# Opening of the even layer: input weights by quarters between conditioning quarters, fillers on TensorE, R multiplied into x ahead

## The chip, the cores and the metric

The kernel runs on one core of one Trainium2 chip. The metric is device time in microseconds (us). PE is TensorE (PEld its weight loads), DVE VectorE, ACT ScalarE, POOL GpSimd, SP SyncE, which issues the transfers (DMAs).

## The reference

Two layers of a diffusion backbone over 512 latent tokens of 1024 channels, all fp32. What matters here is the start of layer 0:

```python
m_lat = (jax.nn.silu(c) @ mod_w[l] + mod_b[l])[:, None, :]
sh1, sc1, g1, sh2, sc2, g2 = jnp.split(m_lat, 6, axis=-1)
h_lat = rms_norm(x, pre_mix_g[l]) * (1 + sc1) + sh1
m_ctx = jax.nn.silu(c_ctx) @ mod_w[l] + mod_b[l]
...
h_ctx = rms_norm(ctx, pre_mix_g[l]) * (1 + csc1) + csh1
...
pl = jnp.split(h_lat @ w_in, EVEN_OFFSETS, axis=-1)   # q, kv, rope key, gla q, k, v, gates, output gate
pc = jnp.split(h_ctx @ w_in, EVEN_OFFSETS, axis=-1)
```

So the first projections need, for each of eight chunks of 128 channels, the norm of x (over all chunks) and two conditioning vectors (a scale A and a shift S for x, A0c and S0c for the 256 context tokens), which come out of a product of c with a 1024 x 2048 part of `mod_w`.

## The kernel before

Activations lie transposed, channels on partitions, tokens along the free dimension: x is eight tiles of 128 x 512, ctx eight of 128 x 256. An fp32 product is made of three fp32r products: every operand is split into a high part (`hi`, a cast on ScalarE) and a low part (`lo`, the rest, a subtraction on VectorE or GpSimd), and `kstep` adds hi x hi, lo x hi and hi x lo. Weights come as units of 128 x 1024 (512 KB), each holding all eight k-chunks of 128 outputs; `unit` loads a few units ahead into four `raw` buffers and splits them.

The opening runs from the first loads to the last product with the first four units: rg (rope keys and gate ranks), kv, gq0 and gq1. Its products are written as `wave(ks, w, js)`: for k-chunks ks, for the latent (w = 0) or context tokens (w = 1), units js. The conditioning product is done in four quarters q, each for the two k-chunks 2q and 2q + 1 of x: `cond_load(q)` loads 2 MB in eight pieces (tiles `mw`, or `raw` for the first quarter and the end of the fourth), `cond` multiplies them (32-column products), `cond_done` copies the row out (tile `mrow`), turns it with two thin products against `sel` and makes A, S, A0c, S0c of two chunks. Then `latent(c)` and `context(c)` make `hl` and `hc` with `modulate`: VectorE makes x * A * R, ScalarE adds S for the high part, VectorE makes the low part. R is the rms factor of x, spread over partitions by PE (`rms_sum`, `rms_spread`; the power is GpSimd's).

Before, the four units are loaded whole after the first conditioning quarter, and each conditioning product of the later quarters is cut in two, with waves between the halves.

The class `ordered` keeps the instructions of an engine in the order in which they are written while its `on` is set: before, PE and SP in the opening. Everywhere else a scheduler decides the order from the program and its own model. SP issues transfers in order, and an issue waits where its buffer is not yet free; PSUM has two `big` buffers and four `one` buffers.

Behind the opening come gk0 and gk1 (`two`), beside which VectorE sums modulation vectors from `mraw` loads (`mod_steps`, tiles `macc`), then a run of thin products: the sum of squares of kv (`kvq`), the doubling of the rope key (`tk`, `dup`), four gates (`gin` x `wz` in `log_gates`, 32 rows), then units q0, q1, gv0 to gv3, gr0 and on. The log gates `lg` feed the linear attention: scans on VectorE (`bf`, `cb`), exponentials on ScalarE and products on GpSimd (`q`, `ek`, `ke`, `ec`), beside GpSimd's weight splits.

## Time and profile before

| | |
|---|---|
| median of 3 runs | 1357.37 us (1352.23 to 1358.7) |
| profiled execution | 1357.05 us, span 1355.2 us |
| busy, share of the span | PE 96%, PEld 78%, DVE 54%, ACT 40%, POOL 39% |
| opening's input products, first to last | 22.16 to 66.8 us |
| mean granted clock over the span | 0.985 |

The granted clock has two levels: 1.00 is 2.4 GHz, 0.50 is 1.2 GHz. In timeline rows x is the number of instructions merged, and the bracket is the idle time of the engine ahead of the row and what ended it. An fp32 (not fp32r) product counts twice there.

### The profile page before, as it was taken

The page shows a single profiled execution, that of the slowest core. Times are in us where ns is not written, and L with a number is a line of the kernel's source. Part 1 is how long each engine was busy: PE and PEld are TensorE (multiplying, and loading weights), DVE is VectorE, ACT ScalarE, POOL GpSimd, SP SyncE. Part 2 cuts the span into 40 slices and gives each one's busy share as a digit, 9 for nine tenths or more (in the row PEclk, how much of TensorE's full clock was granted, in tenths as well). Part 3 has the DMA queues.
Part 4 walks back from the last instruction along what each step waited for, and adds up shares of the span by engine and source line. Part 5 has one row for each costly group of instructions (what it writes and reads, how often), then busy time and mean ns, then how long its engine had stood idle before and what let it go on. Part 6 is the DMA issues. An engine that isn't in the chain of part 4 may idle for free.

```text
span 1355.2 us, 19529 instructions
## 1 busy us (share of the span) xinstructions
PE 1301.6 (96%) x7602; PEld 1052.9 (78%) x7602; DVE 734.6 (54%) x1132; ACT 546.9 (40%) x964; POOL 522.4 (39%) x352
## 2 busy tenths in 40 slices
PE   5999899899999999999999999999999999999997
PEld 3767777686889777777888996567998888888886
DVE  5787478875366779787212477337563333331113
ACT  4417446666454333333323351225444333332221
POOL 2334844210332444444222283744153444442223
PEclk8999999999999999999999999999999999999999
DMA  9891210002314676665332317613123233323321
GB/s 312 290 334 38 78 63 16 1 17 94 110 38 158 208 250 214 232 222 185 99 97 91 105 55 209 167 44 96 46 80 93 94 93 95 108 89 97 89 83 63
DMA packets 69628, 164.41 MB, mean 121 GB/s; under 512 B 7424, under 2 KB 19136, under 8 KB 69536
## 3 DMA queue, kind: packets, MB, share of 16 engines
q1 hardware_dynamic: 68960, 162.64, 37.5%
q8 instruction: 60, 0.98, 0.3%
q10 hardware_dynamic: 576, 0.52, 0.1%
q14 instruction: 32, 0.26, 0.1%
HBM read 159.65 MB, written 3.49 MB: 120 GB/s over the span
## 4 chain that ended last, share of the span: by engine, by line
PE 64%; DVE 3%; DMA 1%; POOL 1%; ACT 1%; issue 0%; SPq 0%; POOLq 0%; ACTq 0%; DVEq 0%
PE one L114 43%; PE big L114 22%; DVE z L1273 1%; POOL a L187 1%; DMA us<-du 0%; DMA raw<-in_W 0%; DVE ty L1501 0%; DVE z L1497 0%; DVE yf L217 0%; DVE z L1496 0%; DMA du<-u 0%; DVE y L497 0%; DVE ty L1504 0%; ACT yf L216 0%; DVE wo L187 0%
## 5 line engine op out<-in xcount | busy, mean ns | idle before, releaser
L187 POOL TENSOR_TENSOR lo<-raw,hi 128x1024 fp32r<-128x1024 f32 (+2 forms) x172 | 340.5, 1984 | 563.9 <-ACT hi L185 491.9
L185 ACT CAST hi<-raw 128x1024 fp32r<-128x1024 f32 (+2 forms) x238 | 174.1, 765 | 220.6 <-issue 141.8
L114 PE MATMUL big<-h,hi 128*128 128x512 f32 (+1 forms) x928 | 257.1, 359 | 1.6 <-ACT h L523 1.6
L114 PE MATMUL one<-h,hi 128*128 128x512 f32 x704 | 221.8, 391 | 0.0
L114 PE MATMUL one<-act,hi 128*128 128x512 f32 (+1 forms) x748 | 209.1, 364 | 0.0
L114 PEld LDWEIGHTS big<-h,hi 128*128 128x128 f32 x928 | 167.0, 191 | 31.5 <-issue 4.2
L114 PE MATMUL big<-h,lo 128*128 128x512 f32 (+1 forms) x464 | 164.7, 358 | 0.0
L114 PEld LDWEIGHTS one<-h,hi 128*128 128x128 f32 x704 | 132.2, 188 | 30.7 <-ACT cv L1217 2.5
L114 PEld LDWEIGHTS one<-act,hi 128*128 128x128 f32 x748 | 135.3, 189 | 22.3
L323 DVE SCALAR_TENSOR_TENSOR macc<-mraw,ccs,macc 128x512 f32<-128x512 f32 x140 | 144.2, 1070 | 14.3 <-DMA mraw<-in_MW 14.3
L114 PE MATMUL one<-h,lo 128*128 128x512 f32 x352 | 137.0, 389 | 0.0
L114 PE MATMUL one<-act,lo 128*128 128x512 f32 (+1 forms) x374 | 136.1, 364 | 0.0
L187 DVE TENSOR_TENSOR lo<-raw,hi 128x512 fp32r<-128x512 f32 (+1 forms) x66 | 46.2, 707 | 131.7 <-ACT hi L185 131.7
L114 PEld LDWEIGHTS big<-h,lo 128*128 128x128 f32 x464 | 88.4, 191 | 12.4
L114 PEld LDWEIGHTS one<-act,lo 128*128 128x128 f32 x374 | 70.6, 189 | 11.2
L114 PEld LDWEIGHTS one<-h,lo 128*128 128x128 f32 x352 | 66.1, 188 | 13.4
L1218 DVE SCALAR_TENSOR_TENSOR cv<-big,vec,cv 128x511 f32<-128x511 f32 x22 | 16.5, 748 | 99.2 <-ACT cv L1217 99.0
L422 DVE TENSOR_TENSOR ysq<-ysq,ysq 128x256 f32<-128x256 f32 (+1 forms) x39 | 21.8, 560 | 86.8 <-ACT ysq L420 86.8
L217 DVE TENSOR_TENSOR act<-cv,act 128x512 fp32r<-128x512 f32 x44 | 50.3, 1143 | 18.4 <-ACT act L216 17.9
L1222 ACT ACTIVATE cv<-cv 128x512 f32<-128x512 f32 x44 | 27.8, 632 | 78.6 <-DVE cv L1220 78.5
L418 ACT ACTIVATE y<-one,m 128x512 f32<-128x512 f32 (+1 forms) x27 | 17.4, 643 | 85.2 <-PE one L114 85.2
L216 ACT CAST act<-cv 128x512 fp32r<-128x512 f32 x44 | 27.3, 620 | 53.8 <-DVE cv L1223 53.8
(363 smaller groups left out, 2186.2 us busy)
## 6 DMA issues: line engine op xcount, KB each, us to landing
raw<-in_W SPq DMA_DIRECT2D x173, 512.0 KB, 3.5
mraw<-in_MW SPq DMA_DIRECT2D x160, 256.0 KB, 5.2
raw<-in_W SPq DMA_DIRECT2D x16, 384.0 KB, 3.0
mw<-in_MW SPq DMA_DIRECT2D x22, 256.0 KB, 6.7
us<-du SPq DMA_DIRECT2D x20, 270.0 KB, 6.4
x<-in_xT SPq DMA_DIRECT2D x16, 256.0 KB, 5.3
raw<-in_MW SPq DMA_DIRECT2D x10, 256.0 KB, 5.4
out<-x SPq DMA_DIRECT2D x12, 128.0 KB, 2.2
```

Of the source, the lines that this page charges most:

```text
L114: i = f(*a, **k)
L185: ac.copy(h, r)
L187: (ve if dv else po).tensor_tensor(out=l, in0=r, in1=h.bitcast(F32), op=ALU.subtract)
L216: ac.copy(h, src)
L217: (eng or ve).tensor_tensor(out=l, in0=src, in1=h.bitcast(F32), op=ALU.subtract)
L323: ve.scalar_tensor_tensor(out=a, in0=r, scalar=ccs[:, 2 * k:2 * k + 1], in1=a, op0=ALU.mult, op1=ALU.add)
L418: ac.activation(ys[d][:, ts], o[:, ts], AF.Copy, scale=gp[:, d:d + 1])
L422: ve.tensor_tensor(out=s[:, ts], in0=s[:, ts], in1=a[:, ts], op=ALU.add)
L1218: ve.scalar_tensor_tensor(out=c[:, 1:], in0=g[:, :511], scalar=wj(0), in1=c[:, 1:], op0=ALU.mult, op1=ALU.add)
L1222: ac.activation(c, c, AF.Gelu)
L1273: f = lambda: ve.scalar_tensor_tensor(out=z[:, o], in0=u[:, i], scalar=w_(n, t), in1=z[:, o], op0=ALU.mult, op1=ALU.add)
```

## The change

The four first units are loaded in quarters of 128 KB (256 columns, two k-chunks), a quarter of each behind each quarter of the conditioning matrix, and split the same way (rg's low part on VectorE, the others' on GpSimd). `quarter(q, m)` does what belongs to a conditioning quarter: vectors, splits, and `parts`, in which ScalarE makes the high part as x * A + S in one pass and VectorE makes x * A + S and the low part; R has been multiplied into x before. The conditioning products of a quarter are no longer cut. PE gets fillers whose result is not used (`busy`, and four products of x with ones): NB gives their numbers. The row copy `mrow` goes from VectorE to ScalarE, the context's sum of squares from GpSimd to VectorE. All five engines keep the written order in the opening. The first 16 columns of `vec` are loaded alone, ahead of x, the rest behind the identity.

```diff
+NB = (4, 1, 6, 10, 8)
...
-    pe, sy = ordered(pe), ordered(sy)
+    ve, ac, po, pe, sy = (ordered(e) for e in (ve, ac, po, pe, sy))
...
-    sy.dma_start(out=vec, in_=V)
+    sy.dma_start(out=vec[:, 0:16], in_=V[:, 0:16])
     x0 = load_x()
     sy.dma_start(out=ident, in_=KD[:, 0:128])
+    sy.dma_start(out=vec[:, 16:], in_=V[:, 16:])
...
-            if q == 0 or (q == 3 and k >= 6):
-                if k % 2 == 0:
-                    r = T(wp, "raw", 1024, bufs=4)
-                t = r[:, (k % 2) * 512:(k % 2 + 1) * 512]
-            else:
-                t = E(s="mw") if q == 1 else Wd(s="mw")[:, 0:512]
+            t = E(s="mw") if q == 0 or (q == 2 and k >= 6) else Wd(s="mw")[:, 0:512]
...
-        i = ve.tensor_copy(r, m[:, 0:256]).ins
-        if q == 0:
-            marks["ve", 0, 0] = i
+        ac.copy(r, m[:, 0:256])
...
+    def rows_load(q):
+        for j, n in enumerate(first):
+            if q == 0:
+                raws.append(T(wp, "raw", 1024, bufs=4))
+            o = int(UOFF[UIX[n]])
+            sy.dma_start(out=raws[j][:, q * 256:(q + 1) * 256],
+                         in_=W[o:o + 128 * 1024].rearrange("(p w) -> p w", w=1024)[:, q * 256:(q + 1) * 256])
+
+    def rows_split(q, js):
+        for j in js:
+            if q == 0:
+                us.append(([T(wp, "hi", 1024, F32R, bufs=3)], [T(wp, "lo", 1024, F32R, bufs=3)], 1024) if j == 0 else
+                          ([E(F32R, s="wf") for _ in range(2)], [E(F32R, s="wf") for _ in range(2)], 512))
+            h, l = wsl(us[j], q * 256, 256)
+            split_to(h, l, raws[j][:, q * 256:(q + 1) * 256], po if j else ve)
+
+    def parts(src, A, S, cs, dst):
+
+        for c in cs:
+            ac.activation(dst[c][0], src[c], AF.Identity, scale=A[:, c:c + 1], bias=S[:, c:c + 1])
+        for c in cs:
+            h, l = dst[c]
+            ve.tensor_scalar(out=src[c], in0=src[c], scalar1=A[:, c:c + 1], scalar2=S[:, c:c + 1],
+                             op0=ALU.mult, op1=ALU.add)
+            ve.tensor_tensor(out=l, in0=src[c], in1=h.bitcast(F32), op=ALU.subtract)
+
+    def quarter(q, m, more=()):
+
+        for c in more:
+            ve.tensor_tensor(out=x0[c], in0=x0[c], in1=Rs[0], op=ALU.mult)
+        vectors = cond_done(q, m)
+        vectors(A0, S0, 0)
+        cs = (2 * q, 2 * q + 1)
+        hl.extend((C(F32R, s="hl"), C(F32R, s="hl")) for _ in cs)
+        rows_split(q, (0,))
+        parts(x0, A0, S0, cs, hl)
+        vectors(A0c, S0c, 1)
+        rows_split(q, (1, 2, 3))
...
+    def context(cs):
+        for c in cs[::2]:
+            p = hcs.pop(0)
+            hc.extend([t[:, i * NX:(i + 1) * NX] for t in p] for i in range(2))
+        parts(cin, A0c, S0c, cs, hc)
...
+    ac.on = ve.on = po.on = True
+    ps = [big(), big(), one(), one()]
+    fz = C(F32R, s="fz")
+    ve.tensor_copy(fz, ones[:, 0:1].broadcast_to([128, NT]))
+
+    def busy(n):
+
+        for _ in range(n):
+            pe.matmul(ps[1][:, NT:2 * NT], lhsT=fz[:, 0:128], rhs=fz, start=True, stop=True)
+
     ts = [cond_load(0)]
+    rows_load(0)
+    ts.append(cond_load(1))
+    rows_load(1)
     m0 = one()
-    cond(m0, ts[0], range(4))
     o = one()
-    rms_sum([sumsq(x0, NT)], NT, o)
-    cond(m0, ts[0], range(4, 8))
-    Rs.append(C(s="R"))
-    rms_spread(o, NT, D)
-    marks["ac", 1, 0] = ac.copy(Rs[0], o).ins
-    cond_done(0, m0)
-    (marks["ac", 2, 0], marks["ve", 1, 0]), (_, marks["ve", 2, 0]) = latent(0), latent(1)
-    us = [unit(n, 0, nl=3 - i, both=True) for i, n in enumerate(first)]
-    ps = [big(), big(), one(), one()]
-    ts.append(cond_load(1))
+    sq = sumsq(x0, NT)
+    for c in range(KC - NB[0], KC):
+        pe.matmul(ps[1][:, NT:2 * NT], lhsT=ones, rhs=x0[c], start=True, stop=True)
+    for k in range(KC):
+        cond(m0, ts[0], (k,))
+        busy(NB[1])
+        if k == 1:
+            rms_sum([sq], NT, o)
+        if k == 4:
+            Rs.append(C(s="R"))
+            rms_spread(o, NT, D)
+            ac.copy(Rs[0], o)
+    sel = cvec("sel", 4)
+    for i in range(2):
+        ve.tensor_tensor(out=sel[:, 2 * i:2 * i + 2], in0=ident[:, 32 * i:32 * i + 2],
+                         in1=ident[:, 64 + 32 * i:66 + 32 * i], op=ALU.add)
+    quarter(0, m0, (0, 1))
+    busy(NB[2])
+    for c in range(2, KC):
+        ve.tensor_tensor(out=x0[c], in0=x0[c], in1=Rs[0], op=ALU.mult)
     for c in range(KC):
         sy.dma_start(out=cin[c], in_=cT[c])
-    for q in range(2, 4):
+    for q in (2, 3):
         ts.append(cond_load(q))
+        rows_load(q)
+    hcs = [hpair() for _ in range(4)]
+    st["load"] = st["split"] = len(first)
     sy.on = False
...
-    wave(k01, 0, (0,))
-    wave(k01, 0, (1,))
-    cond(m1, ts[1], range(0, 4))
-    wave(k01, 0, (2,))
-    cond(m1, ts[1], range(4, 8))
-    sq = sumsq(cin, NX, po)
-    wave((0,), 0, (3,))
-    cond_done(1, m1)
-    for c in k23:
-        latent(c)
-    wave((1,), 0, (3,))
+    wave(k01, 0, (0, 1, 2))
+    cond(m1, ts[1], range(KC))
+    quarter(1, m1)
+    wave(k01, 0, (3,))
+    busy(NB[3])
+    sq = sumsq(cin, NX)
     o = one()[:, 0:NX]
-    m2 = one()
-    cond(m2, ts[2], range(0, 4))
+    wave(k23, 0, (0, 1))
     rms_sum([sq], NX, o)
-    wave(k23, 0, (0,))
+    wave(k23, 0, (2, 3))
     Rs.append(C(n=NX, s="R"))
     rms_spread(o, NX, D)
     ac.copy(Rs[1], o)
-    for c in (*k01, *k23):
-        context(c)
-    cond(m2, ts[2], range(4, 8))
-    wave(k23, 0, (1,))
-    cond_done(2, m2)
-    for c in k45:
-        latent(c)
-        context(c)
+
+    def normed_in(cs):
+        for c in cs:
+            ve.tensor_tensor(out=cin[c], in0=cin[c], in1=Rs[1], op=ALU.mult)
+
+    normed_in(k01)
+    context(k01)
+    m2 = one()
+    cond(m2, ts[2], range(KC))
+    quarter(2, m2)
+    normed_in((*k23, *k45, *k67))
+    context(k23)
+    busy(NB[4])
+    wave(k01, 1, (0, 1))
     m3 = one()
-    wave(k23, 0, (2, 3))
-    cond(m3, ts[3], range(0, 4))
-    wave((*k01, *k23), 1, (0, 1))
-    cond(m3, ts[3], range(4, 8))
-    wave(k45, 0, (0,))
-    cond_done(3, m3)
-    wave(k45, 0, (1,))
-    for c in k67:
-        latent(c)
-        context(c)
+    wave(k45, 0, (0, 1))
+    cond(m3, ts[3], range(KC))
+    quarter(3, m3)
     wave(k45, 0, (2, 3))
+    wave(k23, 1, (0, 1))
+    context(k45)
+    context(k67)
     wave(k45, 1, (0, 1))
-    for k in k67:
-        wave((k,), 0, (0, 1))
-        wave((k,), 1, (0, 1))
+    wave(k67, 0, (0, 1))
+    wave(k67, 1, (0, 1))
     wave(k67, 0, (2, 3))
-    pe.on = False
+    pe.on = ac.on = ve.on = po.on = False
     p, pkv = ps[0][:, 0:NA], ps[1][:, 0:NA]
     wz = C(s="wz")
     sy.dma_start(out=wz[64:96, :], in_=WZ)
```

The first place is PE's first wave. `big_248`, `big_249` and `one_250` are the outputs of rg, kv and gq0; `one_307` is the second conditioning quarter. Before:

```order
L114 MATMUL big_248<-hl_205,hi_218 128x512
L114 MATMUL big_248<-hl_205,lo_219 128x512
L114 MATMUL big_248<-hl_206,hi_218 128x512
L114 MATMUL big_249<-hl_200,wf_224 128x512
L114 MATMUL big_249<-hl_200,wf_226 128x512
L114 MATMUL big_249<-hl_201,wf_224 128x512
L114 MATMUL big_249<-hl_205,wf_224 128x512
L114 MATMUL big_249<-hl_205,wf_226 128x512
L114 MATMUL big_249<-hl_206,wf_224 128x512
L114 MATMUL one_307<-mw_252,c_15_113 32x256 x2
L114 MATMUL one_307<-mw_254,c_15_113 32x256 x2
```

Now `big_121`, `big_122` and `one_123` are those outputs, and `fz` is a filler's operand:

```order
L115 MATMUL one_171<-mw_141,c_15_114 32x256 x2
L115 MATMUL big_122<-fz_125 128x512
L115 MATMUL one_171<-sel,mrow_243 128x4 x2
L115 MATMUL big_122<-fz_125 128x512 x6
L115 MATMUL big_121<-hl_250,hi_254 128x512
L115 MATMUL big_121<-hl_250,lo_255 128x512
L115 MATMUL big_121<-hl_251,hi_254 128x512
L115 MATMUL big_122<-hl_250,wf_267 128x512
L115 MATMUL big_122<-hl_250,wf_269 128x512
L115 MATMUL big_122<-hl_251,wf_267 128x512
L115 MATMUL one_123<-hl_250,wf_273 128x512
```

The six fillers stand between the turn and the first wave, which goes chunk by chunk over three units, where before rg was done for both chunks and then kv, with half a conditioning quarter behind.

The second place is PE's gates' run, behind gk1. `rs` is the rms factor of kv, `macc` a modulation sum, `gin` x `wz` a gate. Before, ahead of q0 (`one_1007`):

```order
L114 MATMUL big_899<-tk_630,dup_632 128x512
L114 MATMUL big_899<-tk_630,dup_632 128x256
L114 MATMUL one_924<-macc_764,ones 32x512
L114 MATMUL one_924<-macc_765,ones 32x512
L114 MATMUL big_880<-ident,rs_889 128x128 x6
L114 MATMUL one_935<-ident,mrow_927 128x64 x4
L114 MATMUL one_1007<-hl_200,hi_1010 128x512
L114 MATMUL one_1007<-hl_200,lo_1011 128x512
L114 MATMUL one_1007<-hl_201,hi_1010 128x512
```

Now:

```order
L115 MATMUL big_987<-tk_718,dup_720 128x512
L115 MATMUL big_987<-tk_718,dup_720 128x256
L115 MATMUL big_968<-ident,rs_977 128x128 x6
L115 MATMUL big_1055<-gin_722,wz_716 128x512
L115 MATMUL big_1055<-gin_722,wz_716 128x256
L115 MATMUL big_1063<-gin_722,wz_716 128x512
L115 MATMUL big_1063<-gin_722,wz_716 128x256
L115 MATMUL one_1012<-macc_852,ones 32x512
L115 MATMUL big_1071<-gin_722,wz_716 128x512
L115 MATMUL big_1071<-gin_722,wz_716 128x256
L115 MATMUL one_1012<-macc_853,ones 32x512
L115 MATMUL big_1079<-gin_722,wz_716 128x512
```

All four gates stand ahead of q0. Before they stood within q0, and between and behind the parts of q1 and gv0.

The third place is ScalarE behind gk1: `za` are the gates' activations, `qs` and `qsq` the copies of the outputs of q0 and q1. Before:

```order
L806 COPY qs_1046<-one_1007 128x512
L808 ACTIVATE qsq_1048<-one_1007 128x512
L185 CAST hi_1053<-raw_823 128x1024
L789 ACTIVATE za_978<-za_978 128x768
L806 COPY qs_1081<-one_1050 128x512
L808 ACTIVATE qsq_1083<-one_1050 128x512
L185 CAST hi_1166<-raw_1008 128x1024
L788 ACTIVATE za_986<-big_983,vec 128x768
L789 ACTIVATE za_986<-za_986 128x768
L788 ACTIVATE za_994<-big_991,vec 128x768
L789 ACTIVATE za_994<-za_994 128x768
L795 ACT_TABLE_LOAD
```

Now:

```order
L115 ACTIVATE za_1082<-za_1082 128x768
L115 ACT_TABLE_LOAD
L115 ACTIVATE za_1058<-za_1058 128x768
L115 ACTIVATE za_1066<-za_1066 128x768
L115 ACTIVATE za_1074<-za_1074 128x768
L115 CAST kvh_1839<-kvn_985 128x768
L115 ACTIVATE za_1082<-za_1082 128x768
L115 CAST kh_1853<-krd_990 64x768
L115 CAST kh_1857<-krd_990 64x768
L115 COPY qs_1134<-one_1095 128x512
L115 ACTIVATE qsq_1136<-one_1095 128x512
```

The last two gates' activations, and the table load behind them, stood behind the copies of q1 and stand ahead of those of q0.

## Rows read from the trace of the kernel before

**Rows 1.** Windows: length; busy (instructions) PE, PEld, DVE, ACT, POOL; clock; DMA.

```profile
22.16:66.80 44.64, 42.45 (x261) 30.86 (x262) 30.31 (x62) 18.92 (x35) 16.84 (x14) 0.89 0.91 299
86.50:113.90 27.40, 26.80 (x105) 17.18 (x103) 18.04 (x27) 11.11 (x16) 7.42 (x4) 0.88 0.52 180
```

**Rows 2.** Timeline of TensorE in the opening: start, us, operation, count, idle before.

```profile
15.63 1.69 PE L114 MATMUL one<-raw,c 128*32 128x256 f32 x16
17.25 1.16 PE L114 MATMUL one<-ident,rs 128*128 128x128 f32 x8
18.25 0.51 PE L114 MATMUL one<-sel,mrow 128*128 128x4 f32 x4
...
22.16 0.80 PE L114 MATMUL big<-hl,hi 128*128 128x512 f32 x1 [3.41 <-ACT hl L259]
...
47.27 1.07 PE L114 MATMUL one<-mw,c 128*32 128x256 f32 x16
...
64.05 2.91 PE L114 MATMUL one<-hl,wf 128*128 128x512 f32 x12
```

**Rows 3.** Windows of single clock levels; PEclk stands before the DMA share.

```profile
21.34:28.16 6.82, 5.42 (x12) 3.55 (x12) 6.69 (x7) 3.97 (x7) 4.65 (x3) 0.50 1.06 351
...
38.40:41.80 3.40, 3.40 (x17) 2.48 (x20) 0.12 (x1) 0.37 (x1) 0.63 (x1) 0.50 1.08 349
...
154.46:157.80 3.34, 3.34 (x9) 2.61 (x8) 0.00 (x0) 0.00 (x0) 3.34 (x3) 0.50 0.52 157
```

**Rows 4.** Timeline of TensorE in the gates' run and linear attention.

```profile
86.50 1.40 PE L114 MATMUL big<-ones,kvq 128*128 128x1 f32 x12
87.82 1.55 PE L114 MATMUL big<-tk,dup 64*128 64x512 f32 x4
89.31 1.66 PE L114 MATMUL one<-macc,ones 128*32 128x512 f32 x2
...
100.35 2.84 PE L114 MATMUL big<-gin,wz 32*128 32x512 f32 x8
...
110.86 1.55 PE L114 MATMUL big<-gin,wz 32*128 32x512 f32 x4
...
142.39 0.50 PE L114 MATMUL big<-lo,hl 128*128 128x512 f32 x1 [0.61 <-POOL lo L187]
...
153.88 0.50 PE L114 MATMUL one<-hl,lo 128*128 128x512 f32 x1 [3.03 <-POOL lo L187]
```

**Rows 5.** Timeline of VectorE in the opening.

```profile
17.37 0.42 DVE L630 COPY mrow<-one 128x256 f32<-128x256 f32 x1 [1.47 <-PE one L114]
...
19.52 0.97 DVE L640 TENSOR_TENSOR A<-A,vec 128x2 f32<-128x2 f32 x1
```

**Rows 6.** Timeline of ScalarE.

```profile
21.39 1.39 ACT L259 ACTIVATE hl<-x,S 128x512 fp32r<-128x512 f32 x2 [1.26 <-DVE x L258]
...
111.94 1.05 ACT L185 CAST hi<-raw 128x1024 fp32r<-128x1024 f32 x1
...
123.26 1.28 ACT L851 ACT_TABLE_LOAD   x1
124.55 0.44 ACT L851 ACTIVATE eq<-lg 128x256 f32<-128x256 f32 x1
```

**Rows 7.** Timeline of GpSimd.

```profile
23.36 4.65 POOL L187 TENSOR_TENSOR wf<-raw,wf 128x512 fp32r<-128x512 f32 x3 [2.89 <-ACT wf L185]
...
126.75 3.77 POOL L869 TENSOR_TENSOR q<-q,gq 128x512 f32<-128x512 f32 x2 [4.51 <-ACT q L868]
...
150.25 1.27 POOL L947 TENSOR_TENSOR ek<-ek,gk 128x512 f32<-128x512 f32 x1
151.48 2.34 POOL L187 TENSOR_TENSOR lo<-raw,hi 128x1024 fp32r<-128x1024 f32 x1
```

**Rows 8.** Transfers: packets in 24 to 29.7; issue at 41.4, us to landing.

```profile
DMA packets 2128, 2.01 MB, mean 353 GB/s; under 512 B 162, under 2 KB 2128, under 8 KB 2128
...
raw<-in_MW SPq DMA_DIRECT2D x1, 256.0 KB, 6.1
```

33 lines of the change are left out of this document (9 added, 24 removed).

## Prediction

> **What bounds the kernel now.** I read the page first, then windows, then engine timelines. The page has TensorE (PE) busy in nearly every slice of the span, so the time is what PE executes, at whatever clock it is granted, plus its waits. What a change in the opening is worth is read from the stretch it touches, and from the stretches behind it whose order of instructions moves with it.
>
> The window over the opening, from the first product with layer-0 input weights (22.16) to the last (66.8), is 44.64 us, of which PE is busy 42.45 [rows 1]. PE waited 3.41 before that first product for ScalarE's normalized x [rows 2]. The clock windows show two stretches in which the granted clock was 0.50, the 1.2 GHz level: 21.34 to 28.16, after the 3.41 us wait, and 38.4 to 41.8, after waits for conditioning data [rows 3]. At 2.4 GHz a full product is 0.23 us apart from the next (twelve in 2.91 [rows 2]). So the opening loses to idle time and clock, not to a backlog of other engines.
>
> Behind the opening I looked for stalls that could give the time back or add to it. PE waits 0.61 and 3.03 for GpSimd's weight splits at 142.39 and 153.88 [rows 4], and falls to 1.2 GHz from 154.46 for 3.3 us after the second [rows 3].
>
> **The change, part by part.** All times are against the profiled execution: 1357.05 us, span 1355.2, so some 1.9 us lie outside the span; the median of the runs is 1357.37, 0.3 above.
>
> *Start.* The bytes ahead of the last piece of the first conditioning quarter are the same (vec, x, identity, that quarter), so it lands when it did; its products ended at 17.32 [rows 2]. In the new PE order the spread of R (1.16 [rows 2]) stands before the last three pieces, and each piece is followed by a filler. A piece alone costs at most a pair's 0.5; I take 0.45, plus 0.23 for the filler, so three take 2.0, and the row ends near 18.0. ScalarE copies it (VectorE took 0.42 [rows 5]), the turning products take 0.51 [rows 2], three small vectors some 0.3, and one ScalarE pass 0.72 (two in 1.39 [rows 6]): first operand at 20.0. The six fillers after the turn end at 19.0 + 6 x 0.23 = 20.4. First product 20.4 against 22.16. R multiplied into x beforehand takes VectorE's long pass off this chain: ScalarE no longer waits for a product of x, A and R.
>
> *First wave.* It now takes units rg, kv and gq0 in one wave, and the lows of kv and gq0 come from GpSimd one after the other, behind ScalarE's two passes. GpSimd needed 4.65 for three 128x512 splits [rows 7], so 0.78 for a half as wide one if it scales and 1.55 if it does not. I expect 1.5 us of PE waits (bounds 0.5 and 3).
>
> *PE work.* From the window: 44.64 less 2.19 idle, less half of the 8.8 us that PE was busy at 1.2 GHz (5.4 before 28.16, 3.4 from 38.4 [rows 3]), gives 38.0 at 2.4 GHz. None of it is removed.
>
> *Added on PE.* 10 + 8 fillers lie behind the first wave: 18 x 0.23 = 4.1. They cover the chain from a conditioning quarter to its operands, and cost in full where that chain is shorter. Conditioning quarters now stand undivided (two 1.07 halves [rows 2] in one piece), with the copy to ScalarE behind them and nothing between it and the turning products: 0.5 us of wait, three times, 1.5.
>
> *Opening.* 20.4 + 1.5 + 38.0 + 4.1 + 1.5 = 65.5 against 66.8: a gain of 1.3, if the clock stays at 2.4 GHz. Each 3.4 us at 1.2 GHz costs 1.7.
>
> *Loads.* The 16 quarter loads are 128 KB. Loads of 128 KB beside 256 KB ones ran in a stream of 353 GB/s [rows 8], 0.37 us each, so the four units cost 5.9 us spread over the stream. The last conditioning quarter is then due some 1.5 us before its old landing, 47.5 (issued at 41.4, 6.1 to landing [rows 8]), and PE asks for it near 49. No cost, with 2 to 3 us to spare. The Trainium skill speaks against this part ("DMA: Bandwidth & Descriptors", Bandwidth: collect transfers to 1 MiB or more, since 64 KB runs at 138 GB/s). By it the quarters would take up to 15 us, an estimate from that page, and PE would wait some 7 us; the 353 GB/s of the row does not bear it out, because many loads are in flight at once.
>
> *The gates' run.* The order of the later part moves too. In before, PE runs two gate products between parts of the q0 and q1 projections and two after; now all four stand ahead of q0, with the second group of modulation products between them. Window 86.5 to 113.9 (end of gk1 to the last gate not yet done at q1's end) is 27.4 us [rows 1]. The same set in the new order, at 2.4 GHz: 1.4 and 1.5 [rows 4], gates 4 x 1.42 = 5.7 and two modulation products 1.7 (one took 1.66 at 1.2 GHz) [rows 4], spread 1.7 (six products, where the opening's four took 1.16 [rows 2]), transposes 0.5, q0 and q1 48 x 0.23 = 11.0, and waits of 2.7 that the old order filled: for GpSimd's power 1.0, for VectorE's kvn 1.1 (the first gate needs that PSUM buffer), for the last copy 0.6. Sum 26.2. The run has thin products (32 or 64 rows, single columns), and before fell to 1.2 GHz after such ones; I count one more 3.4 us at 1.2 GHz: 27.9, a loss of 0.5.
>
> *Linear attention.* What the early gates buy is on ScalarE and GpSimd. In before the last two gates' activations stand behind q1 on ScalarE, and GpSimd starts its decay products at 126.75 [rows 7], 15.9 after q1's last product (110.86 [rows 4]). Now ScalarE has after q1 only two copies of 0.6, a cast of 1.05 and the table load of 1.28, then two 0.44 exponentials and one longer [rows 6]: 5.2. Before, GpSimd's list up to the split that PE waits for took 126.75 to 153.82, 27.1 [rows 7]. The new list has three more entries ahead of that split, 3.5 (two of 1.27 as at 150.25 [rows 7], and a power of 1.0): 30.6, ready 35.8 after q1. PE is there 39.6 after q1 in before, less two gates and the 0.61 stall 36.0. So the 3.03 and the 0.61 go, and with them the fall of the clock at 154.46 (1.7): a gain of 5.3, with little margin (bounds 2.3, if GpSimd is 3 us late, and 7.6, if the waits of some 2.3 us at the next decay products shrink too).
>
> **Sum.** -1.3 + 0.5 - 5.3 = -6.1: 1350.95 for the profiled execution, 1351.3 on the scale of the median.
>
> **Rivals.**
> *Everything hides.* The turn waits and the first wave's waits vanish (-3.0 more), the gates' run keeps 2.4 GHz (-1.2 instead of +0.5) and the waits at the later decay products go (-2.3): -13.1, 1344. For it: 18 fillers stand where PE would idle. Against: one follows no conditioning copy.
> *The gain is given back in the gates' run.* Three low stretches there (5.1 - 1.2 = +3.9) and one in the opening (-1.3 + 1.7 = +0.4), the 5.3 of linear attention kept: -1.0, 1356. For it: in before the clock fell after both thin runs.
> *Small loads are late.* If a 128 KB load takes as long as a 256 KB one, 0.74, the last quarter is 5.9 later, PE waits some 3.5: 1354.8. Against: the row of 353 GB/s.
> *The slower side: the clock in the opening.* Fillers and undivided conditioning products do not count as enough and PE stays at 1.2 GHz through most of the opening. Each us so spent costs 0.5. The gain of 6.1 is gone at 12.2 us of it, and the kernel is 0.5% slower from 26 us. In before it was 8.8 of 44.6. At 35 us: 1351.3 + 17.5 = 1369.
>
> **Chances.** Half a per cent, 6.8 us, is about what a measurement of this kernel can tell from no change, so faster means below 1350.6. Forecast 0.50, of which 0.21 fall below that line since its own range is 1348 to 1355; everything hides 0.20; given back 0.17; late loads 0.04; slower clock 0.09. Faster 0.21 + 0.20 = 0.41, same 0.29 + 0.17 + 0.04 = 0.50, slower 0.09. Range 1343 to 1358: it takes in the first two rivals with their bounds and leaves out the slow one.
>
> **What would show it.** First input-weight product near 20.4 and last near 65.5; granted clock 1.00 from 25 on; PE idle some 0.5 before each turn of a conditioning quarter, and 1.5 in the first wave; no wait for DMA on conditioning data; a fall of the clock in the gates' run; GpSimd's first decay product 5 after q1 and no wait of PE for the split behind gv3. Wrong if PE shows waits on VectorE or GpSimd in each quarter (two-input VectorE operations that end only as a GpSimd one ends: the small vector of 0.97 at 19.52 [rows 5]), or if the order behind the gates brings a new wait for modulation sums.

## The result and the profile after

The changed kernel takes 1373.7 us (median of 4 runs, 1368.97 to 1376.3), the kernel before 1354.8 (4 runs): ratio 1.0134, 95% interval 1.0109 to 1.016. It is slower by 1.3%, where 1351.3 and a range up to 1358 were forecast. The profiled execution is the fastest of the four (1368.97, span 1367.2, mean clock 0.986; the other three have 0.979 or 0.980), so its trace shows 12.0 of the 18.9 us.

Where they went, by the starts of the same products in both traces: to the first input product +4.3 (22.16 to 26.50); first to last input product +10.5; gk0 and gk1 -0.6; from there to the first product of eq and ek in linear attention, the same work in both, +2.3; all behind that -4.5. In that last stretch, up to the last product, the clock records show 4.0 us at 1.2 GHz against 13.7 before, and a us at that level with PE busy costs half a us. This part is no work of the change: in the runs below the stretch has 7 to 27 us of low clock, and over the sixteen traces of this document it takes 1184.3 to 1193.5 us, on average 1188.3 in the five with before's opening and 1188.7 in the eleven others. Without it the trace has 16.5 of the 18.9 us. So single totals are compared by their intervals, and mechanisms by stretches.

The windows that answer to [rows 1] (columns as there), over the opening and over the run from kv's squares to q1's end:

```profile
26.50:81.80 55.30, 44.98 (x280) 34.38 (x280) 40.09 (x83) 23.02 (x48) 18.18 (x16) 0.91 0.67 219
100.76:135.49 34.73, 31.77 (x107) 19.11 (x106) 30.61 (x41) 18.67 (x23) 7.38 (x3) 0.75 0.58 210
```

In the opening PE is idle for 10.32 us (55.30 less 44.98), against 2.19. The timeline of TensorE has all of it in seven waits, of which five stand here, and the late start (answers to [rows 2, 4]; nearly all lines are L115 now, the helper that keeps the order, so one reads by tiles):

```profile
8.14 6.71 PE L115 MATMUL big<-x,ones 128*128 128x512 f32 x8 [8.14 <-DMA x<-in_xT]
14.78 0.63 PE L115 MATMUL one<-mw,c 128*32 128x256 f32 x4
15.33 0.50 PE L115 MATMUL big<-fz 128*128 128x512 f32 x1
15.76 0.63 PE L115 MATMUL one<-mw,c 128*32 128x256 f32 x4
...
24.44 0.61 PE L115 MATMUL one<-sel,mrow 128*128 128x4 f32 x4
...
26.50 0.50 PE L115 MATMUL big<-hl,hi 128*128 128x512 f32 x1
...
27.80 0.50 PE L115 MATMUL big<-hl,hi 128*128 128x512 f32 x1 [0.57 <-DVE hl L115]
...
34.45 0.61 PE L115 MATMUL one<-sel,mrow 128*128 128x4 f32 x4 [0.52 <-ACT mrow L115]
...
44.13 0.58 PE L115 MATMUL one<-ones,sq 128*128 128x1 f32 x4 [2.58 <-DVE sq L115]
...
67.94 0.38 PE L115 MATMUL big<-hc,hi 128*128 128x256 f32 x1 [1.76 <-DVE hc L115]
...
72.81 0.58 PE L115 MATMUL big<-hc,hi 128*128 128x256 f32 x1 [3.91 <-DVE hc L115]
```

At the start the four products of x with ones, in fp32, hold PE to 14.78. The row of conditioning pieces then goes by 0.98 us a pair of piece and filler (14.78 to 15.76), and PE is busy without a gap up to the turn at 24.44, which was at 18.25 [rows 2]. Taking turns is dear: eight pieces in a row take 1.93 (from 32.00 in the same timeline), 0.24 each, and a filler behind another 0.23.

The clock windows that answer to [rows 3]: two low stretches in the opening, each begun in or behind a wait for VectorE, and one of 17 us in the gates' run, during which PE is busy 93% of the time.

```profile
44.97:48.38 3.41, 3.41 (x10) 2.63 (x9) 0.00 (x0) 0.00 (x0) 0.70 (x1) 0.50 0.44 147
68.86:75.69 6.83, 2.92 (x10) 2.49 (x10) 6.06 (x8) 1.05 (x1) 3.58 (x2) 0.50 0.97 351
109.83:126.89 17.06, 15.88 (x30) 7.12 (x29) 14.89 (x24) 8.99 (x11) 0.00 (x0) 0.50 0.65 236
```

VectorE's timeline shows both long waits. The seven sums of the context stand behind all work of the second quarter. Later two operations on 128x256 take 2.46 and 2.47 where the same ones take 0.40:

```profile
40.40 3.58 DVE L115 TENSOR_TENSOR sq<-sq,sq 128x256 f32<-128x256 f32 x7
...
67.03 0.40 DVE L115 TENSOR_SCALAR cin<-cin,A0c,S0c 128x256 f32<-128x256 f32 x1
67.46 0.42 DVE L115 TENSOR_TENSOR hc<-cin,hc 128x256 fp32r<-128x256 f32 x1
67.80 2.46 DVE L115 TENSOR_SCALAR cin<-cin,A0c,S0c 128x256 f32<-128x256 f32 x1
70.29 2.47 DVE L115 TENSOR_TENSOR hc<-cin,hc 128x256 fp32r<-128x256 f32 x1
72.68 0.40 DVE L115 TENSOR_SCALAR cin<-cin,A0c,S0c 128x256 f32<-128x256 f32 x1
```

GpSimd's timeline at that place: the low parts of gk0 and gk1, two splits of about 2.5, from 67.46 to 72.48.

```profile
67.46 5.02 POOL L115 TENSOR_TENSOR lo<-raw,hi 128x1024 fp32r<-128x1024 f32 x2 [0.44 <-ACT hi L115]
```

Behind the opening, the timelines of TensorE, ScalarE and GpSimd have one of three waits in the gates' run (the others are 0.61 for `rs` and 1.18 for `kvn`), the beginning of GpSimd's decay products, and the one wait that is left in linear attention (3.64 in two before [rows 4]):

```profile
112.31 1.91 PE L115 MATMUL one<-macc,ones 128*32 128x512 f32 x2 [1.18 <-DVE macc L115]
...
143.89 0.21 ACT L115 ACTIVATE et<-bf 128x4 f32<-128x4 f32 x1 [4.11 <-DVE bf L115]
...
144.70 1.36 POOL L115 TENSOR_TENSOR q<-q,gq 128x512 f32<-128x512 f32 x1 [4.51 <-ACT q L115]
...
172.07 0.50 PE L115 MATMUL one<-hl,lo 128*128 128x512 f32 x1 [0.80 <-POOL lo L115]
```

### The profile page after: what moved, and what is told of

It reads as the page before. It is cut to its first block, busy times and chain, and to the rows that moved or that the text cites. A ratio compares the mean times of both kernels' runs of the same rounds, so it can differ in the third digit from the quotient of the medians.

```text
span 1367.2 us, 19656 instructions
## 1 busy us (share of the span) xinstructions
PE 1313.1 (96%) x7642; PEld 1059.0 (77%) x7642; DVE 754.0 (55%) x1152; ACT 551.3 (40%) x976; POOL 516.7 (38%) x353
## 3 DMA queue, kind: packets, MB, share of 16 engines
q1 hardware_dynamic: 70832, 162.65, 37.2%
## 4 chain that ended last, share of the span: by engine, by line
PE 64%; DVE 3%; POOL 1%; DMA 1%; ACT 1%; issue 0%; SPq 0%; POOLq 0%; DVEq 0%; ACTq 0%
PE one L115 42%; PE big L115 21%; DVE z L115 1%; DVE ty L115 1%; POOL a L115 1%; DMA us<-du 0%; DVE y L115 0%; DVE yf L115 0%; POOL rs L115 0%; DMA du<-u 0%; ACT yf L115 0%; ACT h L115 0%; DVE lo L115 0%; DVE u L115 0%; DVE uo L115 0%
## 5 line engine op out<-in xcount | busy, mean ns | idle before, releaser
L115 POOL TENSOR_TENSOR lo<-raw,hi 128x1024 fp32r<-128x1024 f32 (+2 forms) x171 | 340.4, 1995 | 547.4 <-ACT hi L115 506.3
L115 ACT CAST hi<-raw 128x1024 fp32r<-128x1024 f32 (+2 forms) x240 | 174.8, 762 | 205.5 <-issue 143.7
L115 PE MATMUL big<-h,hi 128*128 128x512 f32 (+1 forms) x928 | 255.6, 358 | 1.8 <-ACT h L115 1.8
L115 PE MATMUL one<-h,hi 128*128 128x512 f32 x704 | 221.8, 391 | 0.0
L115 PE MATMUL one<-act,hi 128*128 128x512 f32 (+1 forms) x748 | 209.3, 364 | 0.0
L115 PEld LDWEIGHTS big<-h,hi 128*128 128x128 f32 x928 | 165.7, 189 | 31.9 <-issue 4.2
L115 PE MATMUL big<-h,lo 128*128 128x512 f32 (+1 forms) x464 | 163.8, 357 | 0.0
L115 PEld LDWEIGHTS one<-h,hi 128*128 128x128 f32 x704 | 132.2, 188 | 30.8 <-ACT cv L115 2.5
L115 DVE SCALAR_TENSOR_TENSOR macc<-mraw,ccs,macc 128x512 f32<-128x512 f32 x140 | 145.4, 1076 | 14.6 <-DMA mraw<-in_MW 14.5
L115 PEld LDWEIGHTS one<-act,hi 128*128 128x128 f32 x748 | 135.3, 189 | 22.5
L115 PE MATMUL one<-h,lo 128*128 128x512 f32 x352 | 137.0, 389 | 0.0
L115 PE MATMUL one<-act,lo 128*128 128x512 f32 (+1 forms) x374 | 136.1, 364 | 0.0
L115 DVE TENSOR_TENSOR lo<-raw,hi 128x512 fp32r<-128x512 f32 (+1 forms) x69 | 47.1, 690 | 131.3 <-ACT hi L115 131.3
L115 PEld LDWEIGHTS big<-h,lo 128*128 128x128 f32 x464 | 87.7, 189 | 12.3
L115 DVE SCALAR_TENSOR_TENSOR cv<-big,vec,cv 128x511 f32<-128x511 f32 x44 | 32.9, 748 | 95.0 <-ACT cv L115 94.2
L115 PEld LDWEIGHTS one<-act,lo 128*128 128x128 f32 x374 | 70.6, 189 | 11.0
L115 PEld LDWEIGHTS one<-h,lo 128*128 128x128 f32 x352 | 66.1, 188 | 13.3
L115 DVE TENSOR_TENSOR ysq<-ysq,ysq 128x256 f32<-128x256 f32 (+1 forms) x39 | 21.9, 561 | 86.5 <-ACT ysq L115 86.5
L115 POOL TENSOR_TENSOR rs<-ms,mhalf 128x2 f32<-128x2 f32 (+2 forms) x23 | 21.9, 950 | 110.1 <-DVE ms L115 92.1
L115 DVE TENSOR_TENSOR act<-cv,act 128x512 fp32r<-128x512 f32 x44 | 52.5, 1192 | 18.5 <-ACT act L115 17.9
L115 ACT ACTIVATE cv<-cv 128x512 f32<-128x512 f32 x44 | 27.9, 634 | 83.8 <-DVE cv L115 83.7
L115 ACT ACTIVATE y<-one,m 128x512 f32<-128x512 f32 (+1 forms) x27 | 17.4, 643 | 85.1 <-PE one L115 85.1
```

The costliest lines, as they stand in the source:

```text
L115: i = f(*a, **k)
```

## The experiments

Fourteen kernels, each measured beside the kernel before. Times are in us, from one profiled execution each: the start of the first input product; the opening from there to the start of its last product; the run from kv's squares to the start of the last product of q1 or the gates; linear attention from there to the first product of eq and ek. The last two hold the same work only in sum. Low is time at 1.2 GHz by the clock records. Where the clock falls differs between traces of the same instructions, so a difference of a us or two between two single traces decides nothing: up to the first input product b1, b2 and g1 are the changed kernel unedited, and it starts at 24.6 to 26.5 in the four.

| kernel | ratio to before (95%) | first product | opening, low | run, low | linear attention | run and linear attention |
|---|---|---|---|---|---|---|
| before | 1 | 22.2 | 44.4, 9.4 | 28.6, 6.8 | 51.3 | 79.9 |
| changed | 1.0134 (1.0109 to 1.016) | 26.5 | 54.9, 10.2 | 34.5, 17.1 | 47.7 | 82.2 |
| a1 | 1.0165 (1.0133 to 1.0197) | 27.5 | 55.6, 13.7 | 33.5, 17.1 | 47.0 | 80.5 |
| a3 | 1.0127 (1.0097 to 1.0157) | 23.6 | 56.8, 13.7 | 35.0, 23.9 | 46.6 | 81.6 |
| b1 | 1.0138 (1.012 to 1.0156) | 26.1 | 53.6, 6.8 | 35.1, 20.5 | 46.6 | 81.7 |
| b2 | 1.0112 (1.0083 to 1.0142) | 24.6 | 52.4, 10.2 | 35.3, 23.9 | 47.5 | 82.8 |
| c1 | 1.0094 (1.0078 to 1.011) | 24.3 | 47.1, 0 | 35.3, 23.9 | 46.6 | 81.9 |
| g1 | 1.0185 (1.0161 to 1.0209) | 26.2 | 56.5, 13.7 | 35.8, 13.7 | 50.1 | 85.9 |
| c3 | 1.0139 (1.0121 to 1.0157) | 23.1 | 47.1, 0 | 35.3, 17.1 | 51.8 | 87.0 |
| c4 | 1.0145 (1.0124 to 1.0165) | 23.6 | 48.1, 6.8 | 35.8, 17.1 | 50.1 | 85.9 |
| f1 | 1.0104 (1.0079 to 1.0128) | 23.7 | 47.1, 0 | 23.9, 3.4 | 61.5 | 85.4 |
| e2 | 1.0161 (1.0139 to 1.0183) | 25.9 | 47.5, 3.4 | 37.2, 17.1 | 58.6 | 95.8 |
| d1 | 1.0004 (0.9981 to 1.0028) | 21.7 | 43.4, 9.2 | 32.6, 17.1 | 47.1 | 79.7 |
| e1 | 1.0086 (1.0063 to 1.0109) | 22.5 | 43.6, 6.8 | 28.8, 0 | 58.4 | 87.2 |
| e3 | 1.0061 (1.004 to 1.0082) | 22.2 | 43.4, 6.8 | 28.8, 0 | 58.0 | 86.8 |
| e4 | 0.9978 (0.9964 to 0.9992) | 22.1 | 43.4, 9.1 | 25.8, 0 | 48.7 | 74.5 |

### The start: a1 and a3

```diff
-NB = (4, 1, 6, 10, 8)
+NB = (0, 1, 6, 10, 8)      a1
+NB = (0, 0, 6, 10, 8)      a3
```

a1: 

> The changed kernel without the four products of x with ones at its start (first entry of NB 0). Theory backlog: those products ran from 8.14 to 14.78 at 0.85 us a pass and held the first conditioning products back, whose first piece had landed at 11.80. Without them the eight pieces with their fillers (0.98 us a pair) and R's products (0.95 + 1.05) start near 12 and end near 22; first input product near 23.8 instead of 26.5, the kernel some 2.7 us faster. Rival clock: those products are what brought PE to the full clock, which the records show at 1.00 from 14.25; without them the pieces run at 0.50, the first input product comes no earlier than 26, and nothing is gained.

a3: 

> The changed kernel without any filler ahead of the first turn (first two entries of NB 0). Theory backlog: PE follows the landings again (the last piece lands at 17.07), the turn is near 18.3, the first input product near 20.2 instead of 26.5: 6.3 us faster if the clock behind it stays at 1.00. Rival clock: with PE waiting for pieces the granted clock falls for 3 to 7 us behind the first product, as in the kernel before from 21.34 to 28.16, and 2 to 3.5 of the 6.3 are given back.

Each theory had half, and neither total differs from the changed kernel's beyond the intervals. a1's timeline of TensorE:

```profile
11.81 1.07 PE L115 MATMUL one<-mw,c 128*32 128x256 f32 x4 [11.81 <-DMA mw<-in_MW]
12.81 0.80 PE L115 MATMUL big<-fz 128*128 128x512 f32 x1
...
27.48 0.50 PE L115 MATMUL big<-hl,hi 128*128 128x512 f32 x1
```

The pieces begin 3 us earlier (14.78 in the changed kernel), but a piece takes 1.07 and a filler 0.80 instead of 0.63 and 0.50. The clock records begin at 20.8, with 1.00; by these times the clock is at its lower level up to there. What is gained is lost again. Without any start filler (a3) the backlog goes, pieces still run slowly to 20.4, where its records begin, and the first product is at 23.6: 2.9 of the 6.3 us that the backlog theory promised, 1.5 behind before.

### The two waits in the opening: b1, b2 and c1

```diff
     # b1: ahead of the second turn, on GpSimd
+    sq = sumsq(cin, NX, po)
     quarter(1, m1)
-    sq = sumsq(cin, NX)
     # b2: low parts of gk0 and gk1
-    po.tensor_tensor(out=l, in0=r, in1=h.bitcast(F32), op=ALU.subtract)
+    with tc.issue_after(vl):      # the last VectorE operation of the opening
+        ve.tensor_tensor(out=l, in0=r, in1=h.bitcast(F32), op=ALU.subtract)
```

b1: 

> The changed kernel with the context's sum of squares made by GpSimd ahead of the second turn, instead of by VectorE behind it. Theory written order: PE waited 2.58 at 41.5 for these sums only because they stood on VectorE behind all work of the second quarter (7 additions in 3.58 from 40.40, the context had landed by 30.49). Ahead of the turn they are done near 36, the wait goes, and the low clock that followed it (3.41 us from 44.97) goes or moves: the opening's end 2.6 to 4.3 us earlier. Rival contention: the seven GpSimd additions run beside VectorE's products of x and R and its normalized parts and lengthen them; the second quarter's first product (38.67) then comes 1 to 2 us later and half of the gain is lost.

b2: 

> The changed kernel with the low parts of gk0 and gk1 made on VectorE behind the context's parts, instead of on GpSimd beside them. Theory contention: the two VectorE operations of 2.46 and 2.47 us (0.41 in other places) stood against GpSimd's two splits from 67.46 to 72.48; without these they take 0.41 each, PE's waits of 1.76 and 3.91 us and the low clock from 68.86 go: 6 to 7 us off the opening's end (81.8 to about 75). Rival: VectorE is merely late, since it works through its list in written order; then the operations stay long or PE's wait stays above 3 us.

c1 (b1, b2 and a3): 

> The changed kernel with three edits together: no filler ahead of the first turn, the context's sum of squares early on GpSimd, low parts of gk0 and gk1 on VectorE behind the context. Theory additive: without start fillers the opening's last product began at 80.4, with the low parts on VectorE at 77.0 instead of 81.4; with the wait of 2.6 gone as well 70 to 73; the gates' run stays at 33 to 35 us, since its order is as changed; the kernel 8 to 10 us faster than the changed one and still some 8 slower than before. Rival: each stretch saved returns as low clock elsewhere in the opening, whose end then stays at 75 or later.

In b1 the wait of 2.58 is gone: written order it was. The first product of the second quarter, 12.2 us behind the kernel's first one in the changed kernel, is 12.4 behind it here (38.48 less 26.06). The contention is real, in b1's timelines of GpSimd (seven sums) and VectorE (six products of x and R, 3.68 in the changed kernel), but mostly hidden there:

```profile
29.91 7.58 POOL L115 TENSOR_TENSOR sq<-sq,sq 128x256 f32<-128x256 f32 x7
```

```profile
29.96 6.93 DVE L115 TENSOR_TENSOR x<-x,R 128x512 f32<-128x512 f32 x6
```

The fillers stand before the second quarter's first product, and PE then waits only 0.57 and 0.24 more for `hl`. The opening ends 1.7 us earlier, less than the 2.6 expected at least, and the total shows no gain.

In b2's timeline of VectorE the context's operations are short, since no split stands beside them:

```profile
66.83 0.43 DVE L115 TENSOR_TENSOR hc<-cin,hc 128x256 fp32r<-128x256 f32 x1
67.17 0.41 DVE L115 TENSOR_SCALAR cin<-cin,A0c,S0c 128x256 f32<-128x256 f32 x1
67.61 0.42 DVE L115 TENSOR_TENSOR hc<-cin,hc 128x256 fp32r<-128x256 f32 x1
67.96 0.41 DVE L115 TENSOR_SCALAR cin<-cin,A0c,S0c 128x256 f32<-128x256 f32 x1
```

PE's wait of 3.91 is gone; that of 1.76 stays (67.31 in b2). So contention made the one and plain lateness the other: the theory and its rival split the 5.67. The opening is 2.5 shorter, where 6 to 7 were expected off its end. The Trainium skill has this lock ("SBUF — State Buffer", SBUF: two separate sides: VectorE and GpSimd share a pair of ports, which goes to one of them for a whole instruction while the other stops); the 2.46 and 2.47 agree with it.

In the opening c1 adds up: 47.1, all of it at 2.4 GHz, where 54.9 were. It is still 2.7 longer than before, and 2.2 later at its start. But of the 8 to 10 us expected the total has some 5, and gk0 and gk1 take 22.3 where they took 19.4: PE waits 2.71 for the rope key. The key's product stands on VectorE behind a modulation step that waits for its load and then lasts 2.63, beside another split (timelines of TensorE, VectorE and GpSimd):

```profile
74.49 0.50 PE L115 MATMUL big<-hl,hi 128*128 128x512 f32 x1 [2.71 <-DVE tk L115]
...
70.94 2.63 DVE L115 SCALAR_TENSOR_TENSOR macc<-mraw,ccs,macc 128x512 f32<-128x512 f32 x1 [1.50 <-DMA mraw<-in_MW]
...
70.66 2.37 POOL L115 TENSOR_TENSOR lo<-raw,hi 128x1024 fp32r<-128x1024 f32 x1 [8.25 <-ACT hi L115]
```

In e2, where the split begins only after it (72.59), the same step takes 0.75 and PE does not wait. So by these traces the lock had moved to the next place where the two engines meet; c3, c4 and f1 have the same 2.71.

### The fillers behind the first turn: c3 against c4

c3 is c1 with the gates late (g1's edit, below), c4 the same with `NB = (0, 0, 0, 0, 0)`.

c4: 

> As the run before, and without any filler (24 fewer behind the three later turns, 0.23 us each at the full clock, 5.5 us). Theory fillers cost: PE has real work or short waits of about 1.5 us there, so the opening ends 3 to 5 us earlier than with them. Rival fillers hold the clock: without them the granted clock falls in the opening for another 7 us or more, and its end is no earlier.

The windows of the opening, c3's and then c4's:

```profile
23.06:70.13 47.07, 42.25 (x278) 31.60 (x278) 37.06 (x76) 23.20 (x48) 19.98 (x21) 1.00 0.71 229
```

```profile
23.62:71.71 48.09, 41.69 (x260) 30.45 (x260) 36.85 (x76) 23.09 (x48) 19.94 (x21) 0.93 0.69 221
```

In these two traces the rival holds: the fillers (18 of the 24 stand in these windows) keep the clock at 1.00, with 6.8 us of low clock without them, and cost nearly what they save, 1.0 us net. The totals do not tell the two apart. Before has the low clock and is shorter still.

### The gates: g1, c3, f1, d1

```diff
     # g1, c3: gates 0 and 2 behind q0, 1 and 3 behind q1
-    log_gates((0, 2, 1, 3))
+        log_gates(((0, 2), (1, 3))[i], r)      # in the loop over q0 and q1, r its last product
     # f1, besides: R's sum behind piece 4 and its spread behind piece 8; tk between gk0's and gk1's low parts
-    mod_steps(MS[2])                           # moved behind q1
     # d1: the kernel before, q0 behind all four gates
+        with tc.issue_after(g):                # g: the last gate's product
+            proj(p, u, hl)
```

g1: 

> The changed kernel with the order of the gates of the kernel before: two gate products behind q0, two around the beginning of gv0, all eight modulation products ahead of q0; the opening is as changed. Theory clock: the four gates and modulation products in one run are what held the clock at 0.50 for 17 us; apart, the low stretches there are 7 us in all and the run from gk1's end to q1's end is about 4 us shorter; of that the later decay products give back 3 (wait of 3 us for the split behind gv3, as before): the kernel 1 to 2 us faster, or the same. Rival: the low clock comes from what the opening did to the alignment, not from the order; then the run is as long as it was and the kernel is 3 us slower.

c3: 

> The three edits of the run before, and the gates in the order of the kernel before. With the changed opening the late gates left a wait of 4.5 us for VectorE's modulation sums and 13.7 us of low clock. Theory order: four gates and two modulation products in one run are what holds the clock low (in the run with VectorE's low parts PE waited only 0.6 there and the clock was 0.50 for 23.9 us); with the gates apart and the sums in time, the low clock there is 7 us as before, and the stretch from the squares of kv to q1's end, 34 us in the changed kernel and 24 in before (with two gates fewer inside), comes to 25 to 27. Rival late sums: the modulation loads start 9.4 us later than before (70.8 against 61.3) whatever the order is; PE, which is earlier now, waits longer for the sums, 5 us or more, and the stretch stays above 30.

f1: 

> The changed kernel with five edits: no filler ahead of the first turn, R's sum behind the fourth conditioning piece and R's spread behind the eighth, as before; the context's sum of squares early on GpSimd; the low part of gk0 on VectorE behind the context and that of gk1 behind the rope key's product; the third stretch of modulation steps written behind q1, so that its sums no longer stand ahead of q0; and the gates near the end of q1, two and two. Theory: the clock rises near 14.5, as before, since four pieces and not the single-column products come first, so that the first input product is at 21.5 to 22.5 instead of 23 to 24; the opening's last product begins near 68; PE does not wait for the rope key (2.71 with both low parts ahead of it); with full q products between the thin ones and no wait for sums the stretch from kv's squares to q1's end has 3 to 7 us of low clock and takes 25 to 28. In sum 8 to 12 us faster than the run with late gates alone (1371.6), that is 1360 to 1364, still slower than before. Rival: the clock at the start rises at 20 or later whatever comes first, and the low clock behind kv's squares stays above 13 us; then 1368 or more.

d1: 

> The kernel before with one edit: q0's products stand behind all four gates, as in the changed kernel (the two modulation products ahead of the gates); its opening is untouched. From the squares of kv to the last of gates and q1 before took 28.6 us, 6.8 of it at 0.50. Theory order: four gates in one run behind other thin products hold the clock at 0.50 for 17 us or more whatever the opening was; the stretch takes 33 to 35 us, linear attention gains 3 to 4, the kernel is 2 to 4 us slower than before. Rival late sums: the low clock of the changed kernel came from its late modulation sums; here these are in time, the stretch takes 28 to 30 us, and the kernel is 3 us faster than before.

g1 missed: with before's order the run is as long as with the changed one, and the kernel slower. Its timeline of TensorE has a reason, a wait for the modulation sums:

```profile
113.52 2.58 PE L115 MATMUL one<-macc,ones 128*32 128x512 f32 x4 [4.53 <-DVE macc L115]
```

c3 has it too (4.49), so there the rival of late sums held. These sums begin late because SP's queue does: in the changed kernel's timeline the first load of gk0 is issued at 62.55, and every modulation load stands behind it. The last line is from SP's waits over that stretch (total, times, longest).

```profile
50.20 0.55 SPq L115 DMA_DIRECT2D tk<-in_KK  x1
62.55 2.81 SPq L115 DMA_DIRECT2D raw<-in_W  x2
...
66.41 1.06 SPq L115 DMA_DIRECT2D mraw<-in_MW  x2
...
SPq L115 <- DVE lo L115: 11.7, 1, 11.7
```

gk0's buffer is rg's, which the quarter loads keep until the last quarter is split; before issued its load at 42.9 and the first modulation load at 57.2. It is not the queue alone: in g1 VectorE stands 6.33 us for PE with sums still to do, and SP up to 10.6 for a split; no run takes these apart. The early gates fill this wait, but b2, c1 and a3, which have no wait for sums in the run, have 23.9 us of low clock in it. d1 takes the sums out of it, being the kernel before with on-time sums. Its windows over the run and linear attention:

```profile
85.67:118.26 32.59, 30.24 (x101) 19.38 (x100) 26.07 (x35) 18.54 (x23) 5.91 (x3) 0.74 0.38 140
118.26:165.38 47.12, 46.92 (x219) 38.65 (x217) 33.93 (x33) 21.04 (x36) 35.49 (x22) 1.00 0.23 74
```

So with four gates in one run the clock is low for 17.1 us with before's opening too. The run is 4.0 longer than before, and linear attention gives 4.2 back: nothing (ratio 1.0004). The expectation had the mechanism and set it 2 to 4 us too dear. Not all of the 17.1 belongs to the gates: 6.8 lie ahead of the first one (95.93), in a row of thin products that before, e1, e3 and e4 have as well. In windows over that row, d1's and e1's, the same instructions have clocks of 0.67 and 1.00 (before 0.80); why they differ stays open.

```profile
85.67:95.93 10.26, 9.55 (x38) 5.35 (x36) 7.23 (x10) 3.02 (x4) 4.17 (x2) 0.67 1.04 378
```

```profile
86.08:94.25 8.17, 6.82 (x39) 3.99 (x37) 7.13 (x10) 3.02 (x4) 4.17 (x2) 1.00 1.01 361
```

In f1 the sums moved away, the run fell to 23.9 with 3.4 of low clock, and the work came back behind it: linear attention took 61.5, and the median, 1368.3, missed the 1360 to 1364 expected. Its start answered another question: R's products came in before's order, and PE's first pieces still ran at the lower pace, to 20.4.

### Gates apart: e1, e2, e3, e4

```diff
     # e1, on the kernel before: one gate behind q0's k-steps 4 and 8 and q1's 2 and 5
+    QK = ((3, 7), (1, 4))
+            if k in QK[i]:
+                gq_(lambda: gate(todo.pop(0)))
     # e2: the same on the changed kernel with f1's start, b1, b2; e4: on the kernel before with
+    QK = ((1, 3, 5, 7), ())
     # e3: e1, and the q products of the first head pair on VectorE
-            po.tensor_tensor(out=q0, in0=q0, in1=q, op=ALU.mult)
+            (ve if i == 0 else po).tensor_tensor(out=q0, in0=q0, in1=q, op=ALU.mult)
```

e1: 

> The kernel before with its four gates one by one between full products: behind q0's fourth and eighth k-step and q1's second and fifth. With all four in one run ahead of q0 the stretch from kv's squares to the last of q1 and the gates took 32.6 us with 17.1 of low clock, and linear attention gave back 4.2. Theory clock by neighbours: a gate between full products leaves the low clock there at 7 us or less, the stretch takes 27 to 30 us, linear attention (51.3 in before, 47.1 with early gates) keeps 3 to 4 of the gain, since ScalarE has the gates' activations done soon after q1: 2 to 5 us faster than before. Rival: what helps linear attention is that the gates are done 10 us before q1's end, and here the last one is not; then it stays at 50 to 51 and the kernel is as before.

e2: 

> The changed kernel with the start and context edits of the run with five edits (no filler ahead of the first turn and R's products as before, sum of squares early, low parts of gk0 and gk1 on VectorE), the modulation steps in their old place, and the four gates one by one between q products as in the run beside it. Theory late sums: the opening's last product begins near 70.5, PE waits about 4.5 us for the second modulation sums, which stand ahead of q0, and the low clock behind that wait is 10 to 17 us: the stretch takes 32 to 35 us, the kernel 1364 to 1368. Rival: only the gates' run made the clock fall; the stretch takes 27 to 30 and the kernel 1357 to 1361.

e3: 

> The kernel before with its gates one by one between q products, and the two decay products of the first head pair (q) on VectorE instead of GpSimd. Theory held off: GpSimd's first instruction behind its split is then a 128x256 subtraction; VectorE's run of two-input operations is 1.4 us longer, and GpSimd's subtraction lasts 10 us or more instead of 0.6; PE's wait stays near 12. Rival that product: the subtraction takes 0.6 to 1.2, the rms power stands early, PE's wait of 12.2 falls below 4, and the kernel is 3 to 5 us faster than before.

e4: 

> The kernel before with all four gates one by one inside q0, behind its second, fourth, sixth and eighth k-step. Theory of the prediction's step (early gates are worth 4 to 5 us where they cost no clock): the stretch from kv's squares to q1's end has 0 to 7 us of low clock and takes 26 to 30 us (32.6 with the gates in one run, two gates fewer inside 28.6 in before), linear attention takes 47 as with early gates: 4 to 6 us faster than before. Rival: VectorE holds GpSimd's first product off here too, linear attention takes 55 or more, and the kernel is 4 us or more slower than before.

In e1 gates between full products leave no low clock (0 us), and yet linear attention took 58.4. GpSimd's timeline, and the line of TensorE's waits over that stretch (total, times, longest):

```profile
132.19 12.08 POOL L877 TENSOR_TENSOR q<-q,gq 128x512 f32<-128x512 f32 x1 [4.78 <-ACT q L876]
```

```profile
PE one L114 <- POOL rs L239: 12.2, 1, 12.2
```

One product that takes 1.36 in e4 lasted 12.08, while VectorE went through its scans and differences without a pause; the power of q's norm (`rs`), for which PE waits, stood behind it. e3 puts another instruction there, and it is held off as well (two subtractions, 1.95 in e4):

```profile
130.82 13.97 POOL L951 TENSOR_TENSOR ek<-bf 128x256 f32<-128x256 f32 x2 [4.02 <-DVE bf L843]
```

So it is VectorE's run and not that product. e2 has the same 12.08 and the late sums as well, as its theory said (4.49 of wait, 17.1 of low clock), and ended above its bounds.

e4 has the gates early and apart. Its windows over the run and linear attention, and the GpSimd product:

```profile
85.35:111.18 25.83, 24.49 (x101) 15.26 (x100) 20.77 (x29) 14.74 (x19) 6.58 (x3) 1.00 0.51 179
111.18:159.89 48.71, 46.93 (x218) 38.65 (x216) 37.36 (x40) 24.64 (x41) 34.19 (x21) 1.00 0.21 64
```

```profile
121.64 1.36 POOL L877 TENSOR_TENSOR q<-q,gq 128x512 f32<-128x512 f32 x1 [3.92 <-ACT q L876]
```

Both gains are there: 74.5 against 79.9. Half of before's 6.8 us of low clock in the run lies in the row ahead of the gates, though, which e4 does not change. e4 is faster than both kernels, with the old opening: 1351.5 against 1354.3 (ratio 0.9978, 0.9964 to 0.9992), 2.9 us and not the 4 to 6 expected.

## Why the prediction was wrong, step by step

- **Start: the step that failed first** (first product at 20.4, measured 26.5). It counted PE as abreast of the landings and priced only the last three pieces. It gave the four products of x no price: they take 6.6 us and end at 14.78, 3 us behind the landing of the first piece (11.81 in a1). It took 0.68 for a piece with its filler, measured 0.98, and eight such pairs stand in a row, not three. a3 got 2.9 us back; most of the rest is the slow pace of the first pieces, and what sets that stays open.
- **First wave and turns** (waits of 1.5 and 3 x 0.5): 0.57 and 0.52, 0.49, 0.49. Right or better.
- **Waits that were not in the sum**: 2.58 for the context's sums, 1.76 and 3.91 for its low parts, 8.25 together. The change keeps VectorE in written order and moves the sums there; the prediction did not ask what stood ahead of them. The contention stood under what would make it wrong, with the right mark, and without a price.
- **Clock in the opening** (none low): 10.2 us low, in which PE was busy 6.3, so 3.2. With 6.1 at the start and 7.3 more of waits than counted, this makes the 16.3 us between 65.5 and 81.8.
- **Fillers** (4.1, cover waits): cost as counted; what they bought is clock (c3, c4), and not enough of it in the changed kernel.
- **Loads** (no cost): right. PE waits for no DMA behind the first piece. The 7 us of wait estimated from the Trainium skill ("DMA: Bandwidth & Descriptors", Bandwidth) did not come. What was missed is the queue behind: gk0's load and with it the modulation loads, 9.3 us later at SP.
- **Gates' run** (27.9, with one low stretch of 3.4): 34.7. The waits agree in sum (2.7 counted, 2.97 measured) with some luck: the 0.6 for the last copy did not come, GpSimd's power cost 0.61 and not 1.0, and 1.18 was a wait for a modulation sum, which the prediction had only among its signs of being wrong. The low clock was 17.1 us, during which PE was busy 15.9, so 7.9 and not 1.7. This term was mis-sized; that thin products bring the clock down was right, and d1 against e1 and e4 shows that it goes by the gates' neighbours.
- **Linear attention** (-5.3): both waits shrank from 3.64 to 0.80 and the low clock went. From the end of the gates' run, as the prediction cut it, to the first product of eq and ek: 52.5 before, 47.5 after, -5.0. The number is right by two errors that cancel. GpSimd's first decay product came 9.2 us after q1 (144.70 less 135.48), not 5: ScalarE waited 4.11 for VectorE's scan, which the chain left out. GpSimd's list up to the split then took some 27 and not 30.6.

Together: 16.3 at the opening's end, 6.8 in the gates' run and 0.3 in linear attention, less 0.7 in gk0 and gk1 (by the prediction's windows) and 4.5 behind, make the 18 us between the 1350.95 forecast for the profiled execution and its 1368.97.

Of the rivals, the gains given back in the gates' run happened, larger than priced. The slower side came, but the clock in the opening has only 3.2 us of it; the rest is PE's own backlog, VectorE's list, its lock with GpSimd, and the clock in the gates' run.
